# RMSNorm and matmul on one core: weight chunks on the queue of the token loads, first pair of tiles multiplied chunk by chunk

## The chip, the cores and the metric

The kernel runs on one core of one Trainium2 chip. The metric is device time in microseconds (us), the median of several executions. The engines that matter are TensorE (PE in the profile, with its weight loads as PEld), VectorE (DVE), ScalarE (ACT), GpSimd (POOL) and SyncE (SP), which here only issues transfers. "ACTq" and "SPq" are the queues on which ACT and SP issue theirs.

## The reference

```
batch, seq, dim, out_dim = 16, 1024, 512, 768
rms = np.sqrt(np.mean(x ** 2, axis=-1, keepdims=True) + eps)
x_norm = x / rms * gamma
return np.matmul(x_norm, weight).astype(np.float32)
```

`x` holds 16,384 tokens of 512 numbers, `weight` is 512 x 768, all in float32.

## The kernel before, in words

**Tiles.** 128 tokens make a tile, two tiles a pair (64 pairs, numbered j), two pairs a group (32 groups, numbered g). One load brings a group (`xt`, 1 MB), one store takes a group's results away (`ot`, 1.5 MB). The 512 of `dim` is K = 4 chunks of 128; the weight comes in four chunks of 128 rows (`w_f`, 384 KB each). The 768 output columns are two matmuls, of 512 and of 256.

**A pair.** `cast(j)` on POOL turns the pair into bf16 (`xb`). `squares(j)` on ACT sums the squares of both tiles and takes the root (`rms`); DVE then takes the reciprocal (`rstd`). `transposes(j)` is eight transposes on PE into PSUM (`tp`) and one copy by DVE to SBUF (`xT`). `matmuls(j)` multiplies: for each of the two tiles t, for each chunk k, two matmuls with `xT` held and the scaled weight `w_bf` streamed, added up in a PSUM tile `ops`. When a tile is finished, its PSUM is multiplied by `rstd` into `ot`: by ACT for t = 0 (L110), by DVE for t = 1 (L112). This multiplication is called the eviction here.

**The weight.** gamma is loaded as a row (`g_row`), transposed on PE and copied (`g_sb`); four DVE instructions (L148) then scale each weight chunk by gamma into `w_bf` in bf16. Each waits for its chunk to land.

**What sets the order.** Every engine runs its instructions in the order in which the program is written; nothing reorders them. All loads of `x` and all stores are issued by SP; the gamma row and the four weight chunks are issued by ACT (L123, L126). The main loop (L151) issues, for pair j: the load of the group six ahead (j even), `cast(j+2)`, `squares(j+1)`, `transposes(j+1)`, `matmuls(j)`, and after an odd j the store of the group. So pair 1 is squared and transposed ahead of `matmuls(0)`. There are eight `xt` buffers, three of `xb`, three of `xT`, two of `tp`, three of `ops` and four of `ot`; a group's first eviction therefore needs the store of the group four before to have landed. Transfers take eight completion semaphores (DMAHW0 to DMAHW7) in turn, so each transfer from the ninth on also waits until the one eight issues before it has landed.

Of the kernel before, what the change touches and what calls it, by code (L numbers as in the profile page):

```python
# [12 lines left out]
F32 = mybir.dt.float32  # L13
# [4 lines left out]
@with_exitstack  # L18
def kernel(
    ctx: ExitStack,  # L20
    tc: tile.TileContext,
    x: bass.AP,
    gamma: bass.AP,
    weight: bass.AP,
    eps: float,
    out: bass.AP,
):
    nc = tc.nc
    P = 128

    x = x.flatten_outer_dims()
    out = out.flatten_outer_dims()
    N, D = x.shape
    _, O = out.shape
    K = D // P
    G = 4
    NG = N // (P * G)
    NP = 2 * NG
    PF = 6
    SPLITS = [(0, 512), (512, O)]  # L40


    xg = x.rearrange("(g p t) d -> g p t d", p=P, t=G)
    og = out.rearrange("(g p t) o -> g p t o", p=P, t=G)

    singles = ctx.enter_context(tc.tile_pool(name="singles", bufs=1))
    xin = ctx.enter_context(tc.tile_pool(name="xin", bufs=PF + 2))
    xbp = ctx.enter_context(tc.tile_pool(name="xb", bufs=3))
    junk = ctx.enter_context(tc.tile_pool(name="junk", bufs=2))
    stats = ctx.enter_context(tc.tile_pool(name="stats", bufs=4))  # L50
    xt_pool = ctx.enter_context(tc.tile_pool(name="xt", bufs=3))
    tpsum = ctx.enter_context(tc.tile_pool(name="tpsum", bufs=2, space=bass.MemoryType.PSUM))
    opsum = ctx.enter_context(tc.tile_pool(name="opsum", bufs=3, space=bass.MemoryType.PSUM))
    outp = ctx.enter_context(tc.tile_pool(name="out", bufs=4))

    x_tiles, xb_tiles, rstd_tiles, xT_tiles, o_tiles = {}, {}, {}, {}, {}

    def load(g, parts=1):
        xt = xin.tile([P, G, D], F32, name="xt")
        x_tiles[g] = xt  # L60
        n = G // parts
        for i in range(parts):
            nc.sync.dma_start(out=xt[:, i * n:(i + 1) * n, :], in_=xg[g, :, i * n:(i + 1) * n, :])

    def xpair(j):
        return x_tiles[j // 2][:, 2 * (j % 2):2 * (j % 2) + 2, :]

    def cast(j):
        xb = xbp.tile([P, 2, D], BF16, name="xb")
        xb_tiles[j] = xb  # L70
        nc.gpsimd.tensor_copy(out=xb, in_=xpair(j))  # L71

    def squares(j):
        ssq = stats.tile([P, 2], F32, name="ssq")
        for t in range(2):
            jk = junk.tile([P, D], BF16, name="jk")
            nc.scalar.activation(out=jk, in_=xpair(j)[:, t, :], func=AF.Square,  # L77
                                 accum_out=ssq[:, t:t + 1])
        rms = stats.tile([P, 2], F32, name="rms")
        nc.scalar.activation(out=rms, in_=ssq, func=AF.Sqrt, scale=1.0 / D, bias=eps_sb)  # L80
        rstd = stats.tile([P, 2], F32, name="rstd")
        nc.vector.reciprocal(out=rstd, in_=rms)  # L82
        rstd_tiles[j] = rstd

    def transposes(j):
        xb = xb_tiles.pop(j)
        tp = tpsum.tile([P, 2, K, P], BF16, name="tp")
        for t in range(2):
            for k in range(K):
                nc.tensor.transpose(out=tp[:, t, k, :], in_=xb[:, t, k * P:(k + 1) * P], identity=ident)  # L90
        xT = xt_pool.tile([P, 2, K, P], BF16, name="xT")
        nc.vector.tensor_copy(out=xT, in_=tp)  # L92
        xT_tiles[j] = xT

    def matmuls(j):
        g, h = j // 2, j % 2
        if h == 0:
            o_tiles[g] = outp.tile([P, G, O], F32, name="ot")
        ot = o_tiles[g]
        xT = xT_tiles.pop(j)  # L100
        rstd = rstd_tiles.pop(j)
        for t in range(2):
            ops = opsum.tile([P, 2, 512], F32, name="ops").rearrange("p a b -> p (a b)")
            for k in range(K):
                for lo, hi in SPLITS:
                    nc.tensor.matmul(out=ops[:, lo:hi], lhsT=xT[:, t, k, :], rhs=w_bf[:, k, lo:hi],  # L106
                                     start=(k == 0), stop=(k == K - 1))
            dst = ot[:, 2 * h + t, :]
            if t == 0:
                nc.scalar.mul(out=dst, in_=ops[:, :O], mul=rstd[:, t:t + 1])  # L110
            else:
                nc.vector.tensor_single_scalar(out=dst, in_=ops[:, :O], scalar=rstd[:, t:t + 1],  # L112
                                               op=mybir.AluOpType.mult)

    def store(g, lo=0, hi=G):
        nc.sync.dma_start(out=og[g, :, lo:hi, :], in_=o_tiles[g][:, lo:hi, :])

    with tc.manual_schedule():
        nc.scalar.preload_act_table(AF.Sqrt)  # L119
        load(0, parts=2)  # L120

        g_row = singles.tile([K, P], F32)
        nc.scalar.dma_start(out=g_row, in_=gamma.rearrange("(ko ki) -> ko ki", ki=P))  # L123
        w_f32 = singles.tile([P, K, O], F32)
        for k in range(K):
            nc.scalar.dma_start(out=w_f32[:, k, :], in_=weight[k * P:(k + 1) * P, :])  # L126
        for g in range(1, PF):
            load(g)

        ident_f = singles.tile([P, P], F32)  # L130
        make_identity(nc, ident_f)
        ident = singles.tile([P, P], BF16)
        nc.vector.tensor_copy(out=ident, in_=ident_f)  # L133
        eps_sb = singles.tile([P, 1], F32)
        nc.vector.memset(eps_sb, float(eps))

        cast(0)
        cast(1)
        squares(0)
        transposes(0)  # L140

        gp = tpsum.tile([P, K], F32, name="tp")
        nc.tensor.transpose(out=gp, in_=g_row, identity=ident_f[:K, :K])  # L143
        g_sb = singles.tile([P, K], F32)
        nc.vector.tensor_copy(out=g_sb, in_=gp)  # L145
        w_bf = singles.tile([P, K, O], BF16)
        for k in range(K):
            nc.vector.tensor_single_scalar(out=w_bf[:, k, :], in_=w_f32[:, k, :], scalar=g_sb[:, k:k + 1],  # L148
                                           op=mybir.AluOpType.mult)

        for j in range(NP):  # L151
            if j % 2 == 0 and j // 2 + PF < NG:
                load(j // 2 + PF)
            if j + 2 < NP:
                cast(j + 2)
            if j + 1 < NP:
                squares(j + 1)
                transposes(j + 1)
            matmuls(j)
            g = j // 2  # L160
            if g == NG - 1:
                store(g, 2 * (j % 2), 2 * (j % 2) + 2)
            elif j % 2:
                store(g)
# [35 lines left out]
```

## Time and profile before

| what | value |
|---|---|
| median of 3 runs | 222.38 us (222.13 to 222.49) |
| the profiled execution | 222.73 us |
| its span, first to last instruction | 221.0 us |
| outside the span | 1.73 us |
| PE busy | 198.6 us (90%) |
| ACT busy | 156.1 us (71%) |
| DVE busy | 116.1 us (53%) |
| POOL busy | 67.3 us (30%) |
| moved by DMA | 85.73 MB, mean 388 GB/s |
| granted TensorE clock, mean | 0.996 |

Times inside the span count from its start. A row of the timeline has the start, the duration, the engine, the line, the operation, the tiles written and read, the shapes, and how many instructions were merged; in brackets stands how long the engine had been idle, and what ended that. Durations of merged rows run from the first start to the last end. A row of the windows view has the busy time and the instruction count of each engine in one stretch of time, then the granted TensorE clock, the busy share of the DMA engines, and the GB/s moved.

### The profile page before, as it was taken

The page shows a single profiled execution, that of the slowest core. Times are in us where ns is not written, and L with a number is a line of the kernel's source. Part 1 is how long each engine was busy: PE and PEld are TensorE (multiplying, and loading weights), DVE is VectorE, ACT ScalarE, POOL GpSimd, SP SyncE. Part 2 cuts the span into 40 slices and gives each one's busy share as a digit, 9 for nine tenths or more (in the row PEclk, how much of TensorE's full clock was granted, in tenths as well). Part 3 has the DMA queues.
Part 4 walks back from the last instruction along what each step waited for, and adds up shares of the span by engine and source line. Part 5 has one row for each costly group of instructions (what it writes and reads, how often), then busy time and mean ns, then how long its engine had stood idle before and what let it go on. Part 6 is the DMA issues. An engine that isn't in the chain of part 4 may idle for free.

```text
span 221.0 us, 4062 instructions
## 1 busy us (share of the span) xinstructions
PE 198.6 (90%) x1508; PEld 130.8 (59%) x1537; DVE 116.1 (53%) x199; ACT 156.1 (71%) x385; POOL 67.3 (30%) x70
## 2 busy tenths in 40 slices
PE   0514999999999999999999999999999999999990
PEld 0302666666666666666666666666666666666660
DVE  0222356655566555665555665556655566555551
ACT  3501577787777887778877778777788777887750
POOL 2440133322333323333233333233332333322000
PEclk9999999999999999999999999999999999999998
DMA  6999379999999999999999999999999999776767
GB/s 199 420 420 425 151 279 395 417 424 423 422 412 428 427 416 429 421 416 420 426 430 426 423 427 429 428 421 426 429 421 425 426 428 415 336 307 291 291 288 285
DMA packets 10108, 85.73 MB, mean 388 GB/s; under 512 B 1124, under 2 KB 1128, under 8 KB 2152
## 3 DMA queue, kind: packets, MB, share of 16 engines
q1 hardware_dynamic: 9504, 83.89, 91.1%
q10 hardware_dynamic: 584, 1.58, 1.8%
q8 instruction: 12, 0.20, 0.3%
q14 instruction: 8, 0.07, 0.1%
HBM read 35.13 MB, written 50.33 MB: 387 GB/s over the span
## 4 chain that ended last, share of the span: by engine, by line
PE 88%; DMA 7%; issue 1%; DVE 1%; ACTq 1%; ACT 0%
PE ops L106 75%; PE tp L90 13%; DMA w_f<-in_weight_dram 7%; ACTq L126 1%; DVE ot L112 0%; DVE w_bf L148 0%; ACT L119 0%
## 5 line engine op out<-in xcount | busy, mean ns | idle before, releaser
L106 PE MATMUL ops<-w_bf,xT 128*128 128x256 bf16 (+1 forms) x995 | 178.4, 328 | 10.3 <-DVE w_bf L148 8.8
L106 PEld LDWEIGHTS <-xT 128*128 128x128 bf16 x1024 | 98.3, 99 | 69.3 <-issue 12.0
L71 POOL CAST xb<-xt 128x1024 bf16<-128x1024 f32 x64 | 66.6, 1042 | 134.6 <-PE tp L90 125.9
L112 DVE TENSOR_SCALAR ot<-ops,rstd 128x768 f32<-128x768 f32 x64 | 65.1, 1018 | 74.3 <-PE ops L106 74.3
L110 ACT ACTIVATE ot<-ops,rstd 128x768 f32<-128x768 f32 x64 | 57.7, 901 | 53.3 <-PE ops L106 53.3
L77 ACT ACTIVATE jk<-xt 128x512 bf16<-128x512 f32 x128 | 78.7, 619 | 3.1 <-DMA xt<-in_x_dram 3.1
L90 PE MATMUL tp<-ident,xb 128*128 128x128 bf16 x512 | 40.3, 223 | 6.8 <-POOL xb L71 6.2
L90 PEld LDWEIGHTS <-xb 128*128 128x128 bf16 x512 | 34.9, 100 | 15.0 <-POOL xb L71 6.7
L92 DVE COPY xT<-tp 128x1024 bf16<-128x1024 bf16 x64 | 43.0, 671 | 0.3 <-PE tp L90 0.3
L77 ACT ACTIVATION_READ_ACCUMULATOR jk<-xt 128x1 f32 x128 | 24.4, 190 | 0.0
L80 ACT ACTIVATE rms<-ssq,eps_sb 128x2 f32<-128x2 f32 x64 | 18.9, 295 | 2.1
L82 DVE RECIPROCAL rstd<-rms 128x2 f32<-128x2 f32 x64 | 10.6, 166 | 15.1 <-ACT rms L80 15.1
L148 DVE TENSOR_SCALAR w_bf<-w_f,g_sb 128x768 bf16<-128x768 f32 x4 | 2.5, 620 | 9.6 <-DMA w_f<-in_weight_dram 9.6
L119 ACT ACT_TABLE_LOAD x1 | 1.3, 1283 | 0.7 <-PEq L181 0.7
L133 DVE CAST ident<-ident_f 128x128 bf16<-128x128 f32 x1 | 0.2, 228 | 1.3 <-POOL ident_f masks.py:199 1.3
masks.py:199 POOL TENSOR_SCALAR_AFFINE_SELECT ident_f<-ident_f 128x128 f32<-128x128 f32 x1 | 0.3, 294 | 0.1
L143 PEld LDWEIGHTS tp<-ident_f,g_row 4*128 4x128 f32 x1 | 0.2, 178 | 0.2 <-issue 0.2
masks.py:197 POOL MEMSET ident_f<- 128x128 f32 x1 | 0.2, 205 | 0.3 <-POOLq L181 0.3
L143 PE MATMUL tp<-ident_f,g_row 4*128 4x4 f32 x1 | 0.3, 264 | 0.0
L181 POOL MEMSET const-float32-0.0<- 128x1 f32 x1 | 0.1, 99 | 0.2 <-issue 0.2
L145 DVE COPY g_sb<-tp 128x4 f32<-128x4 f32 x1 | 0.2, 152 | 0.0
L181 POOL MEMSET const-bfloat16-1.0<- 128x1 bf16 x1 | 0.1, 102 | 0.0
(3 smaller groups left out, 0.3 us busy)
## 6 DMA issues: line engine op xcount, KB each, us to landing
out_dram<-ot SPq DMA_DIRECT2D x31, 1536.0 KB, 9.7
xt<-in_x_dram SPq DMA_DIRECT2D x31, 1024.0 KB, 12.0
w_f<-in_weight_dram ACTq DMA_DIRECT2D x4, 384.0 KB, 12.3
out_dram<-ot SPq DMA_DIRECT2D x2, 768.0 KB, 3.6
xt<-in_x_dram SPq DMA_DIRECT2D x2, 512.0 KB, 4.9
g_row<-in_gamma_dram ACTq DMA_DIRECT2D x1, 2.0 KB
```

What stands on the lines that cost most here:

```text
L71: nc.gpsimd.tensor_copy(out=xb, in_=xpair(j))
L77: nc.scalar.activation(out=jk, in_=xpair(j)[:, t, :], func=AF.Square, accum_out=ssq[:, t:t + 1])
L80: nc.scalar.activation(out=rms, in_=ssq, func=AF.Sqrt, scale=1.0 / D, bias=eps_sb)
L82: nc.vector.reciprocal(out=rstd, in_=rms)
L90: nc.tensor.transpose(out=tp[:, t, k, :], in_=xb[:, t, k * P:(k + 1) * P], identity=ident)
L92: nc.vector.tensor_copy(out=xT, in_=tp)
L106: nc.tensor.matmul(out=ops[:, lo:hi], lhsT=xT[:, t, k, :], rhs=w_bf[:, k, lo:hi], start=(k == 0), stop=(k == K - 1))
L110: nc.scalar.mul(out=dst, in_=ops[:, :O], mul=rstd[:, t:t + 1])
L112: nc.vector.tensor_single_scalar(out=dst, in_=ops[:, :O], scalar=rstd[:, t:t + 1], op=mybir.AluOpType.mult)
L119: nc.scalar.preload_act_table(AF.Sqrt)
L126: nc.scalar.dma_start(out=w_f32[:, k, :], in_=weight[k * P:(k + 1) * P, :])
L148: nc.vector.tensor_single_scalar(out=w_bf[:, k, :], in_=w_f32[:, k, :], scalar=g_sb[:, k:k + 1], op=mybir.AluOpType.mult)
```

## The change

The four weight chunks are no longer issued by ACT but by SP, between the two halves of the first group: SP issues pair 0's tokens, the four chunks, pair 1's tokens, and then the other groups. The gamma row stays on ACT's queue; its transpose and copy now stand ahead of pair 0's. `matmuls(0)` now comes ahead of `squares(1)` and `transposes(1)`, and its loop runs over chunks outside and over the two tiles inside, with both `ops` tiles open at once. For all other pairs the loop runs as before, except that both `ops` tiles are named ahead of the loop.

```
-        for t in range(2):
-            ops = opsum.tile([P, 2, 512], F32, name="ops").rearrange("p a b -> p (a b)")
-            for k in range(K):
-                for lo, hi in SPLITS:
-                    nc.tensor.matmul(out=ops[:, lo:hi], lhsT=xT[:, t, k, :], rhs=w_bf[:, k, lo:hi],
-                                     start=(k == 0), stop=(k == K - 1))
+        acc = [opsum.tile([P, 2, 512], F32, name="ops").rearrange("p a b -> p (a b)") for _ in range(2)]
+
+        order = [(t, k) for k in range(K) for t in range(2)] if j == 0 else \
+                [(t, k) for t in range(2) for k in range(K)]
+        for t, k in order:
+            for lo, hi in SPLITS:
+                nc.tensor.matmul(out=acc[t][:, lo:hi], lhsT=xT[:, t, k, :], rhs=w_bf[:, k, lo:hi],
+                                 start=(k == 0), stop=(k == K - 1))
+            if k < K - 1:
+                continue
...
-        load(0, parts=2)
...
+        x0 = xin.tile([P, G, D], F32, name="xt")
+        x_tiles[0] = x0
+        nc.sync.dma_start(out=x0[:, 0:2, :], in_=xg[0, :, 0:2, :])
         for k in range(K):
-            nc.scalar.dma_start(out=w_f32[:, k, :], in_=weight[k * P:(k + 1) * P, :])
+            nc.sync.dma_start(out=w_f32[:, k, :], in_=weight[k * P:(k + 1) * P, :])
+        nc.sync.dma_start(out=x0[:, 2:4, :], in_=xg[0, :, 2:4, :])
         for g in range(1, PF):
             load(g)
...
+        gp = tpsum.tile([P, K], F32, name="tp")
+        nc.tensor.transpose(out=gp, in_=g_row, identity=ident_f[:K, :K])
+        g_sb = singles.tile([P, K], F32)
+        nc.vector.tensor_copy(out=g_sb, in_=gp)
+
         cast(0)
         cast(1)
         squares(0)
         transposes(0)
 
-        gp = tpsum.tile([P, K], F32, name="tp")
-        nc.tensor.transpose(out=gp, in_=g_row, identity=ident_f[:K, :K])
-        g_sb = singles.tile([P, K], F32)
-        nc.vector.tensor_copy(out=g_sb, in_=gp)
...
             if j + 2 < NP:
                 cast(j + 2)
+            if j == 0:
+                matmuls(0)
             if j + 1 < NP:
                 squares(j + 1)
                 transposes(j + 1)
-            matmuls(j)
+            if j > 0:
+                matmuls(j)
```

On SP, at the head of the program, the transfers stood in this order before (`xt` are token tiles; 128x1024 is a pair, 128x2048 a group; DMAHW names the completion that is waited for):

```order
L63 DMA xt<-in_x_dram 128x1024 x2
L63 DMA xt<-in_x_dram 128x2048
L63 DMA xt<-in_x_dram 128x2048 [waits DMAHW0_49]
L63 DMA xt<-in_x_dram 128x2048 [waits DMAHW1_49]
L63 DMA xt<-in_x_dram 128x2048 [waits DMAHW2_49]
```

At the same place, with the change:

```order
L130 DMA xt<-in_x_dram 128x1024
L132 DMA w_f_87<-in_weight_dram 128x768 x4
L133 DMA xt<-in_x_dram 128x1024
L63 DMA xt<-in_x_dram 128x2048
L63 DMA xt<-in_x_dram 128x2048 [waits DMAHW0_49]
```

The four weight chunks now lie between the two halves of group 0 on this one queue, and pair 1's half and all later groups lie behind them.

On ACT, up to the eviction of pair 1 (`jk,ssq<-xt` are the squares, two to a pair; `rms` is the root; `ot<-ops,rstd` is the eviction of a pair's first tile), the order before:

```order
L123 DMA g_row<-in_gamma_dram 4x128
L126 DMA w_f_90<-in_weight_dram 128x768 x4
L77 ACTIVATE jk,ssq<-xt 128x512 [waits DMAHW0_49]
L77 ACTIVATE jk,ssq<-xt 128x512
L80 ACTIVATE rms<-ssq,eps_sb 128x2 [waits DVE_49,Activation_49]
L77 ACTIVATE jk,ssq<-xt 128x512 [waits DMAHW2_49]
L77 ACTIVATE jk,ssq<-xt 128x512
L80 ACTIVATE rms<-ssq,eps_sb 128x2 [waits Activation_49]
L110 ACTIVATE ot<-ops,rstd 128x768 [waits DVE_49,PE_49]
```

And with the change:

```order
L125 DMA g_row<-in_gamma_dram 4x128
L77 ACTIVATE jk,ssq<-xt 128x512 [waits DMAHW0_49]
L77 ACTIVATE jk,ssq<-xt 128x512
L80 ACTIVATE rms<-ssq,eps_sb 128x2 [waits DVE_49,Activation_49]
L114 ACTIVATE ot<-ops,rstd 128x768 [waits DVE_49,PE_49]
L77 ACTIVATE jk,ssq<-xt 128x512 [waits DMAHW6_49]
L77 ACTIVATE jk,ssq<-xt 128x512
L80 ACTIVATE rms<-ssq,eps_sb 128x2 [waits Activation_49]
```

The eviction of pair 0, which waits for PE, now stands ahead of pair 1's squares and root. On DVE the same happens: the eviction of pair 0 (L116 in the changed file) stands ahead of pair 1's reciprocal and of its copy to `xT`, where it stood behind them.

More of the change, by code (lines that the diff above doesn't have):

```diff
@@ L101, in matmuls @@
         rstd = rstd_tiles.pop(j)
-        for t in range(2):
-            ops = opsum.tile([P, 2, 512], F32, name="ops").rearrange("p a b -> p (a b)")
-            for k in range(K):
-                for lo, hi in SPLITS:
-                    nc.tensor.matmul(out=ops[:, lo:hi], lhsT=xT[:, t, k, :], rhs=w_bf[:, k, lo:hi],
-                                     start=(k == 0), stop=(k == K - 1))
+        acc = [opsum.tile([P, 2, 512], F32, name="ops").rearrange("p a b -> p (a b)") for _ in range(2)]
[7 more added lines that the diff above has]
+                continue
             dst = ot[:, 2 * h + t, :]
             if t == 0:
-                nc.scalar.mul(out=dst, in_=ops[:, :O], mul=rstd[:, t:t + 1])
+                nc.scalar.mul(out=dst, in_=acc[t][:, :O], mul=rstd[:, t:t + 1])
             else:
-                nc.vector.tensor_single_scalar(out=dst, in_=ops[:, :O], scalar=rstd[:, t:t + 1],
+                nc.vector.tensor_single_scalar(out=dst, in_=acc[t][:, :O], scalar=rstd[:, t:t + 1],
                                                op=mybir.AluOpType.mult)
```

## The prediction

> **What bounds the kernel now.** I read the page's chain of waits first: by engine, and then two pieces of the same chain in order of time (start, duration).
>
> ```profile
> span 221.0 us, 4062 instructions
> PE 88%; DMA 7%; issue 1%; DVE 1%; ACTq 1%; ACT 0%
> ```
>
> ```profile
> 2.98 16.52 DMA w_f<-in_weight_dram
> 20.20 3.35 PE ops L106 x10
> ```
>
> The chain has two parts: until 19.50 us the kernel waits for the weight's transfers, and from 20.20 us to near the end it is PE. Next the windows (busy time and count of each engine, granted clock, DMA share, GB/s):
>
> ```profile
> 5.00:24.00 19.00, 8.43 (x40) 4.73 (x41) 4.47 (x10) 5.65 (x16) 5.15 (x5) 1.00 1.01 418
> 24.50:28.50 4.00, 3.95 (x30) 2.56 (x30) 1.86 (x5) 2.42 (x6) 1.76 (x2) 1.00 0.01 2
> 28.50:29.00 0.50, 0.50 (x5) 0.26 (x3) 0.50 (x2) 0.01 (x1) 0.32 (x1) 1.00 0.00 0
> 34.00:100.00 66.00, 65.47 (x508) 43.45 (x517) 38.31 (x66) 52.12 (x131) 22.80 (x22) 1.00 1.01 421
> 100.00:180.00 80.00, 79.37 (x624) 52.96 (x634) 46.48 (x79) 63.59 (x159) 27.09 (x26) 1.00 1.01 426
> ```
>
> From 34 us PE has no gaps to speak of (65.47 of 66.00), but the DMA engines are full as well; between 24.5 and 29 us they stood still. So there is a second bound close behind PE, to which I come back. Now the timeline of the start:
>
> ```profile
> 5.09 0.63 ACT L77 ACTIVATE jk<-xt 128x512 bf16<-128x512 f32 x1 [3.08 <-DMA xt<-in_x_dram]
> 5.12 1.04 POOL L71 CAST xb<-xt 128x1024 bf16<-128x1024 f32 x1 [3.82 <-DMA xt<-in_x_dram]
> 6.22 1.03 PE L90 MATMUL tp<-ident,xb 128*128 128x128 bf16 x8 [6.22 <-POOL xb L71]
> 6.76 1.04 POOL L71 CAST xb<-xt 128x1024 bf16<-128x1024 f32 x1 [0.60 <-DMA xt<-in_x_dram]
> 7.18 0.26 PE L143 MATMUL tp<-ident_f,g_row 4*128 4x4 f32 x1
> 7.29 0.69 DVE L92 COPY xT<-tp 128x1024 bf16<-128x1024 bf16 x1 [0.34 <-PE tp L90]
> 9.22 0.62 DVE L148 TENSOR_SCALAR w_bf<-w_f,g_sb 128x768 bf16<-128x768 f32 x1 [1.17 <-DMA w_f<-in_weight_dram]
> 10.47 2.03 POOL L71 CAST xb<-xt 128x1024 bf16<-128x1024 f32 x2 [2.67 <-DMA xt<-in_x_dram]
> 12.60 0.62 DVE L148 TENSOR_SCALAR w_bf<-w_f,g_sb 128x768 bf16<-128x768 f32 x1 [2.76 <-DMA w_f<-in_weight_dram]
> 14.03 1.04 POOL L71 CAST xb<-xt 128x1024 bf16<-128x1024 f32 x1 [1.52 <-DMA xt<-in_x_dram]
> 16.07 0.62 DVE L148 TENSOR_SCALAR w_bf<-w_f,g_sb 128x768 bf16<-128x768 f32 x1 [2.85 <-DMA w_f<-in_weight_dram]
> 19.53 0.62 DVE L148 TENSOR_SCALAR w_bf<-w_f,g_sb 128x768 bf16<-128x768 f32 x1 [2.83 <-DMA w_f<-in_weight_dram]
> 20.20 3.35 PE L106 MATMUL ops<-w_bf,xT 128*128 128x512 bf16 x10 [2.66 <-DVE w_bf L148]
> 21.03 0.90 ACT L110 ACTIVATE ot<-ops,rstd 128x768 f32<-128x768 f32 x1 [12.64 <-PE ops L106]
> 23.19 0.29 ACT L80 ACTIVATE rms<-ssq,eps_sb 128x2 f32<-128x2 f32 x1
> 23.35 1.06 PE L90 MATMUL tp<-ident,xb 128*128 128x128 bf16 x8
> 24.21 3.00 PE L106 MATMUL ops<-w_bf,xT 128*128 128x512 bf16 x15
> 27.05 0.61 PE L90 MATMUL tp<-ident,xb 128*128 128x128 bf16 x8
> 27.49 2.76 PE L106 MATMUL ops<-w_bf,xT 128*128 128x512 bf16 x16
> 28.10 0.29 ACT L80 ACTIVATE rms<-ssq,eps_sb 128x2 f32<-128x2 f32 x1
> 28.43 0.17 DVE L82 RECIPROCAL rstd<-rms 128x2 f32<-128x2 f32 x1 [0.16 <-ACT rms L80]
> 28.51 0.67 DVE L92 COPY xT<-tp 128x1024 bf16<-128x1024 bf16 x1
> ```
>
> A weight chunk lands every 3.4 us (9.2, 12.6, 16.1, 19.5), while the token loads on the other queue land between them in their own order (5.1, 6.8, 10.5, 14.0). In 3.45 us at 418 GB/s 1.44 MB pass, and a chunk is 0.39 MB: the weight queue gets little more than a quarter of the flow. Two paces of PE show too: from 20.20 to 23.35 us ten matmuls, five pairs of 512 and 256 columns, take 0.63 us a pair; from 27.49 us sixteen take 2.6. The granted clock reads 1.00 in both.
>
> **The change part by part.** I work out when pair 2's matmuls start, since from there on every pair follows at PE's pace:
>
> ```profile
> 30.54 0.38 PE L106 MATMUL ops<-w_bf,xT 128*128 128x512 bf16 x1
> 210.29 5.36 PE L106 MATMUL ops<-w_bf,xT 128*128 128x512 bf16 x31
> ```
>
> The steps 27.49 to 30.54 (pair 3) and 27.49 to 210.29 (pair 62, sixty pairs) both give 3.05 us a pair. Before, pair 2 starts at 27.49.
>
> *Tokens of pair 0.* Nothing ahead of them moves: they are the first transfer on SP before and after. I keep 5.1 us, and cast, transposes and copy end at 7.29 + 0.69 = 7.98. The gamma transpose, put ahead of them on PE and DVE, lies in their idle time; it waits for a 2 KB row that is still the first transfer on ACT's queue. Cover gone, it would cost what its row at 7.18 took, 0.26 us.
>
> *Weights.* On one queue transfers land in the order of issue, as the token loads do. The four chunks, 1.57 MB at 418 GB/s, take 3.76 us: they land at about 6.0, 7.0, 7.9 and 8.9 us. DVE scales them back to back from 7.98 in 0.62 us each; the last is needed at 9.84. So the weight has left the path, and what is late next is the chain of pair 0 itself. Pair 1's tokens land at 10.1 (0.52 MB later) in place of 6.8, group 1 at 12.6 in place of 10.5; both are needed later than that, below. The four issues leave ACT, which idled then, for SP, where later issues shift by about 1.4 us (a store's issue, quoted below, takes 0.35) under transfers that are queued for microseconds: nothing.
>
> *First pair.* PE's first matmul: 7.98 + 0.62 + 0.05 (the DVE end at 20.15 to PE at 20.20) = 8.65. DVE delivers a chunk each 0.62, PE needs 2 x 0.63 for one: PE is the limit, at the slow pace. Tile 0's last pair of matmuls is the seventh; ACT starts its eviction 0.83 after that pair starts (20.20 to 21.03): 8.65 + 6 x 0.63 + 0.83 = 13.26.
>
> *The new wait.* Behind that eviction on ACT now stand pair 1's squares and root, which were done early before, and behind the root stand DVE's reciprocal and `xT` copy, for which PE waits. From eviction to the end of a root is 23.48 - 21.03 = 2.45; from the end of a root at 28.39 to the end of the copy at 29.18 is 0.79, and 0.05 more to PE. So pair 1's matmuls start at 13.26 + 2.45 + 0.79 + 0.05 = 16.55. PE meanwhile ends pair 0 (13.69) and does the transposes of pairs 1 and 2 at the slow 0.86 (23.35 to 24.21): 15.41, and idles 1.1 us. Pair 1's cast is done by 11.2, pair 2's by 13.7: in time. Pair 2's `xT` follows 1.6 us behind pair 1's, well ahead of its use. Pair 2's matmuls start at 16.55 + 3.05 = 19.60.
>
> *Sum.* 27.49 - 19.60 = 7.89 us earlier. The profiled execution took 222.73, of which 1.73 lie outside the span: 214.84. It lay 0.35 above the median, so the median becomes 222.38 - 7.89 = **214.5**. Unknown ends: if PE speeds up soonest, say 3.4 us after 8.65, 1.67 pairs of the seven save 0.3 each, 0.5 in all; if pair 0's tokens land up to 1.0 us sooner, without a second queue's issues beside them, that comes on top: 213.0.
>
> *The second bound.* Stores:
>
> ```profile
> 28.35 0.35 SPq L116 DMA_DIRECT2D out_dram<-ot  x1
> DMA to landing us min/median/max: 6.9/8.6/9.0
> DMA to landing us min/median/max: 13.5/13.6/13.7
> 47.27 0.90 ACT L110 ACTIVATE ot<-ops,rstd 128x768 f32<-128x768 f32 x1 [0.60 <-PE ops L106]
> ```
>
> Store 0 is issued at 28.35, and group 4's first eviction, which needs its buffer, comes at 47.27: a store has 18.9 us to land. It takes 6.9 us at first and 13.7 at most (issues from 28 to 60 us, and from 174 to 182). Before, store 0 met DMA engines that had nothing to do. After, it is issued 7.9 us sooner, at about 20.5, while the loads ahead of it, the same bytes as before, still end at about 24.5. So the stream of stores starts some 4.5 us sooner than the 29 us of before, and everything is asked for 7.9 sooner: landings grow by about 3.5 us, to 17.2 at the worst. That is 1.7 us inside the limit, and at the end the stores drain, so I add nothing.
>
> **The rivals.**
>
> *The stores take over.* Past 18.9 us ACT's eviction waits, then PE, and the pace is DMA's: 2.62 MB a group (1 MB in, 1.5 MB out) at 421 to 426 GB/s is 6.22 to 6.15 us, where PE needs 2 x 3.05 = 6.09. Over the 24 groups with loads that is 1.4 to 3.1 us at worst: 215.9 to 217.6. For it speaks the thin margin, against it that my estimate stays inside.
>
> *PE stays slow.* Before, the fast pace came only after 24.21, with PE busy without a break from 20.20. If the 1.1 us gap ahead of pair 1 puts that off, pair 1 runs at 8 x 0.63 = 5.0 in place of 2.6, and one set of transposes at 0.86 in place of 0.45: 2.9 us, 217.4. Against it: 16.55 lies 7.9 us after 8.65, and PE will have been idle for 1.1 of them. [...]
>
> *The weights land no sooner.* If sharing between transfers does not depend on the queue, the last chunk still lands at 19.5. Its pair of tile 0 starts at 20.20, pair 1's matmuls at 21.03 + 3.29 = 24.32, against 24.21: the gain is gone, and with PE idle again ahead of it, pair 1 runs slow: 5.0 against the 2.84 of before (24.21 to 27.05, where the next transposes began), plus 0.4 for transposes: about 2.6 slower, **225.0**; with the fast pace in time, 222.5, no change. The change loses from the point at which the last chunk lands after 19.4. [...] Against it stand the landing times above, where each queue lands in its own order and two queues share by turns.
>
> **How the numbers follow.** Forecast, 213.0 to 215.5: 0.70. Stores: 0.11. Slow PE: 0.13. Weights no sooner: 0.05, of which 0.03 slower. The rest is unforeseen. The range goes from 213.2, most of the way to the early ends, to 217.4, the slow pair. A difference under 0.2%, 0.44 us, is about what a measurement of this kernel can't tell from no change: faster 0.95, same 0.02, slower 0.03.
>
> **What would show it.** Right: `w_f` landings below 1 us apart and all before 10 us; the first L108 matmul near 8.7; ACT idle until about 13.3, then its first eviction; a PE gap of about 1 us before pair 1 near 16.5, ended by DVE's `xT`; 3.05 us a pair from 19.6 on; no DMA pause near 25 us; store landings up to 17. Wrong: weight waits on DVE past 10 us; L108 matmuls over 0.6 us after 17; evictions that wait for `out_dram`.

## The result, and the profile after

The change makes the kernel faster: 215.03 us against 222.44, a ratio of 0.9686 with an interval of 0.9635 to 0.9736. One of the four executions took 216.75 us and the other three 214.83 to 215.10, and among the experiments below one execution of "PE kept busy" took 216.80 and one of "earlier still" 360.39 us, both left out of their ratios; why these took longer stays open. The profiled execution took 215.10 us, 7.63 less than the one before.

The page after the change, span and chain by engine:

```profile
span 213.2 us, 4093 instructions
PE 92%; DMA 2%; DVE 1%; ACT 1%; POOL 0%; issue 0%
```

The transfers' share of the chain went from 7% to 2%, and PE's from 88% to 92%. The longest early pieces of the chain in order of time:

```profile
0.74 4.84 DMA xt<-in_x_dram
9.06 4.33 PE ops L108 x14
16.71 2.77 PE ops L108 x16
```

What is left of the transfers is the first token load; the weight's transfers are gone from the chain. The same windows as before the change:

```profile
5.00:24.00 19.00, 14.03 (x95) 8.62 (x96) 8.54 (x17) 10.39 (x28) 8.05 (x8) 1.00 1.01 416
24.50:28.50 4.00, 4.00 (x32) 2.58 (x31) 1.77 (x3) 3.37 (x8) 1.04 (x1) 1.00 1.00 421
34.00:100.00 66.00, 66.00 (x524) 43.63 (x523) 38.31 (x66) 52.60 (x132) 22.58 (x22) 1.00 1.01 426
```

PE is busy for 14.03 us of the first window in place of 8.43, and the DMA engines no longer stop between 24.5 and 28.5 us (421 GB/s in place of 2). Now the timeline of the start:

```profile
5.60 0.63 ACT L77 ACTIVATE jk<-xt 128x512 bf16<-128x512 f32 x1 [3.58 <-DMA xt<-in_x_dram]
7.79 0.69 DVE L92 COPY xT<-tp 128x1024 bf16<-128x1024 bf16 x1 [0.34 <-PE tp L90]
8.40 2.20 DVE L156 TENSOR_SCALAR w_bf<-w_f,g_sb 128x768 bf16<-128x768 f32 x4
9.06 4.64 PE L108 MATMUL ops<-w_bf,xT 128*128 128x512 bf16 x16 [1.31 <-DVE w_bf L156]
13.42 0.90 ACT L114 ACTIVATE ot<-ops,rstd 128x768 f32<-128x768 f32 x1 [6.16 <-PE ops L108]
13.54 0.61 PE L90 MATMUL tp<-ident,xb 128*128 128x128 bf16 x8
13.74 1.02 DVE L116 TENSOR_SCALAR ot<-ops,rstd 128x768 f32<-128x768 f32 x1 [3.14 <-PE ops L108]
14.36 0.62 PE L90 MATMUL tp<-ident,xb 128*128 128x128 bf16 x8 [0.21 <-POOL xb L71]
15.57 0.29 ACT L80 ACTIVATE rms<-ssq,eps_sb 128x2 f32<-128x2 f32 x1
15.90 0.17 DVE L82 RECIPROCAL rstd<-rms 128x2 f32<-128x2 f32 x1 [1.14 <-ACT rms L80]
15.98 0.67 DVE L92 COPY xT<-tp 128x1024 bf16<-128x1024 bf16 x1
16.71 2.77 PE L108 MATMUL ops<-w_bf,xT 128*128 128x512 bf16 x16 [1.73 <-DVE xT L92]
19.77 2.76 PE L108 MATMUL ops<-w_bf,xT 128*128 128x512 bf16 x16
202.56 2.65 PE L108 MATMUL ops<-w_bf,xT 128*128 128x512 bf16 x15
```

The four scalings of the weight are one merged row, back to back from 8.40: none waits for a chunk. Pair 0's matmuls run from 9.06, pair 1's start at 16.71 after PE waited 1.73 us for DVE's `xT`, and behind that wait one reads its chain upwards: copy at 15.98, reciprocal at 15.90, root at 15.57, and the eviction at 13.42 ahead of it on ACT. Pair 2 starts at 19.77, pair 62 at 202.56: 3.05 us a pair, as before. Last, landings of the four weight chunks, and of the stores issued from 20 to 52 us and from 165 to 175:

```profile
DMA to landing us min/median/max: 5.3/6.1/6.9
```

```profile
DMA to landing us min/median/max: 9.4/10.2/10.2
```

```profile
DMA to landing us min/median/max: 14.6/14.7/14.9
```

The chunks, issued from 1.2 to 2.6 us, land from 6.5 to 9.5, in the order of issue; the last landed at 19.5 before.

### The profile page after: what moved, and what is told of

The parts are those of the page before. It is cut to its first block, busy times and chain, and to the rows that moved or that the text cites. A ratio compares the mean times of both kernels' runs of the same rounds, so it can differ in the third digit from the quotient of the medians.

```text
span 213.2 us, 4093 instructions
## 1 busy us (share of the span) xinstructions
PE 198.2 (93%) x1537; PEld 129.9 (61%) x1537; DVE 116.0 (54%) x199; ACT 156.0 (73%) x385; POOL 67.2 (32%) x70
## 4 chain that ended last, share of the span: by engine, by line
PE 92%; DMA 2%; DVE 1%; ACT 1%; POOL 0%; issue 0%
PE ops L108 79%; PE tp L90 13%; DMA xt<-in_x_dram 2%; ACT jk L77 1%; POOL xb L71 0%; DVE ot L116 0%; ACT ot L114 0%; DVE xT L92 0%; DVE w_bf L156 0%; ACT rms L80 0%; DVE rstd L82 0%
## 5 line engine op out<-in xcount | busy, mean ns | idle before, releaser
L108 PE MATMUL ops<-w_bf,xT 128*128 128x512 bf16 (+1 forms) x1024 | 178.6, 328 | 3.0 <-DVE xT L92 1.7
L116 DVE TENSOR_SCALAR ot<-ops,rstd 128x768 f32<-128x768 f32 x64 | 65.1, 1018 | 73.9 <-PE ops L108 73.9
L90 PE MATMUL tp<-ident,xb 128*128 128x128 bf16 x512 | 39.5, 220 | 4.4 <-POOL xb L71 4.4
L90 PEld LDWEIGHTS <-xb 128*128 128x128 bf16 x512 | 34.1, 99 | 12.7 <-POOL xb L71 4.7
## 6 DMA issues: line engine op xcount, KB each, us to landing
out_dram<-ot SPq DMA_DIRECT2D x31, 1536.0 KB, 11.1
```

What stands on the lines that cost most here:

```text
L108: nc.tensor.matmul(out=acc[t][:, lo:hi], lhsT=xT[:, t, k, :], rhs=w_bf[:, k, lo:hi], start=(k == 0), stop=(k == K - 1))
L116: nc.vector.tensor_single_scalar(out=dst, in_=acc[t][:, :O], scalar=rstd[:, t:t + 1], op=mybir.AluOpType.mult)
```

## The experiments

All times are medians; the ratio is to the kernel before the change, run beside on the same chip.

**Only the queue.** The kernel before, with the weight chunks on SP's queue.

```
-        load(0, parts=2)
+        nc.sync.dma_start(out=x0[:, 0:2, :], in_=xg[0, :, 0:2, :])
-            nc.scalar.dma_start(out=w_f32[:, k, :], in_=weight[k * P:(k + 1) * P, :])
+            nc.sync.dma_start(out=w_f32[:, k, :], in_=weight[k * P:(k + 1) * P, :])
+        nc.sync.dma_start(out=x0[:, 2:4, :], in_=xg[0, :, 2:4, :])
```

> Only the weight chunks are moved to SP's queue, between the two halves of group 0; the order of the program and the loops stay as before the change. My theory: the gain is the earlier landing of the weights, and the new order of pair 0 adds little. Pair 1's tokens land at about 10.7, its transposes end at 12.7 on PE ahead of pair 0's matmuls, these run from 12.7 to about 17, pair 2's matmuls start at about 20.3 (19.8 to 21.2) against 19.77 with the whole change: 215.5 us (215.0 to 216.5). Rival: the early weights are of use only with pair 0's matmuls ahead of pair 1's tokens, so that most of the gain is missing: 218 or more.

Measured: 215.75 us, 0.9701 (0.967 to 0.9732). Its PE rows at the start:

```profile
12.19 1.03 PE L90 MATMUL tp<-ident,xb 128*128 128x128 bf16 x8 [4.32 <-POOL xb L71]
13.02 4.21 PE L106 MATMUL ops<-w_bf,xT 128*128 128x512 bf16 x16
17.52 2.76 PE L106 MATMUL ops<-w_bf,xT 128*128 128x512 bf16 x16
```

PE idles 4.3 us for pair 1's tokens, which now lie behind the weight, and then runs through pair 0 and pair 1 (17.52) without another wait. The queue alone brings 6.7 of the 7.4 us; the rest of the change adds 0.7 by the medians. The rival falls.

**Only the order.** The changed kernel with the chunks back on ACT's queue.

```
-            nc.sync.dma_start(out=w_f32[:, k, :], in_=weight[k * P:(k + 1) * P, :])
+            nc.scalar.dma_start(out=w_f32[:, k, :], in_=weight[k * P:(k + 1) * P, :])
```

> The new order of the program and the loop over chunks, but the weight chunks stay on ACT's queue. My theory: the chunks land 3.4 us apart up to 19.5 as before, pair 1's matmuls start at about 24.3 against 24.21 before the change, so nothing is gained: 222.5 us, up to 225 if PE runs pair 1 at the slow pace. Rival: the order brings the gain by itself, since PE works on both tiles while it waits: 217 or less.

Measured: 224.42 us, 1.0092 (1.0066 to 1.0118): slower than before the change. Its rows around the last chunk:

```profile
19.44 0.62 DVE L156 TENSOR_SCALAR w_bf<-w_f,g_sb 128x768 bf16<-128x768 f32 x1 [2.83 <-DMA w_f<-in_weight_dram]
21.35 1.91 PE L90 MATMUL tp<-ident,xb 128*128 128x128 bf16 x16
24.24 5.04 PE L108 MATMUL ops<-w_bf,xT 128*128 128x512 bf16 x16 [0.98 <-DVE xT L92]
29.57 2.76 PE L108 MATMUL ops<-w_bf,xT 128*128 128x512 bf16 x16
```

The chunks land as the prediction's third rival has them: the last chunk at 19.4, pair 1 at 24.24 after a PE gap (24.32 worked out there) and at the slow pace, 5.04 us (5.0), so that pair 2 starts at 29.57 against 27.49. It shows both what two queues do to the weight and what the new order costs when the weight is late. What passes on the two queues can be counted in the trace of the kernel before: from 10 to 18 us it has 305 token packets of 8 KB and 282 weight packets of 3 KB, so that the weight gets 0.26 of the bytes.

**Tile by tile.** The whole change, but pair 0 in the usual loop order.

```
-        order = [(t, k) for k in range(K) for t in range(2)] if j == 0 else \
-                [(t, k) for t in range(2) for k in range(K)]
+        order = [(t, k) for t in range(2) for k in range(K)]
```

> The whole change, except that pair 0's matmuls run tile by tile (all chunks of tile 0, then of tile 1) as in all other pairs. My theory: the weights are ready every 0.62 us and PE takes 0.63 us for one chunk of one tile at the slow pace, so PE waits for no chunk in either order; tile by tile, tile 0 is finished 1.65 us sooner (11.8 in place of 13.4), ACT gets to pair 1's squares sooner, and DVE's eviction of tile 1 (13.7 to 14.8) becomes the last ahead of pair 1's reciprocal: pair 1's matmuls at 15.55 in place of 16.71, 1.2 us gained: 213.9 us. Rival: running chunk by chunk is what lets PE start early, and without it PE waits for the weights: slower than the change, 216 or more.

Measured: 213.84 us, 0.9612 (0.9582 to 0.9643), in its profiled execution a span of 211.8 us. Its first eviction and the matmuls of pairs 1 and 2:

```profile
11.77 0.90 ACT L113 ACTIVATE ot<-ops,rstd 128x768 f32<-128x768 f32 x1 [4.57 <-PE ops L107]
15.27 2.77 PE L107 MATMUL ops<-w_bf,xT 128*128 128x512 bf16 x16
18.32 2.44 PE L107 MATMUL ops<-w_bf,xT 128*128 128x512 bf16 x14
```

The eviction comes at 11.77 as worked out, pair 2 at 18.32 in place of 19.77. Running pair 0 chunk by chunk costs 1.45 us at pair 2 and 1.4 of the span; it is not a source of the gain.

**Squares first.** The whole change, with pair 0's evictions (now a function of their own) issued behind pair 1's squares, root and copy.

```
             if j == 0:
-                matmuls(0)
+                acc0 = matmuls(0)
             if j + 1 < NP:
                 squares(j + 1)
                 transposes(j + 1)
+            if j == 0:
+                evict(0, 0, acc0)
+                evict(0, 1, acc0)
```

> The whole change, except that the evictions of pair 0 stand behind pair 1's squares, root, reciprocal and copy on ACT and DVE. My theory: PE's 1.7 us gap ahead of pair 1 is the wait for that root, which stood behind pair 0's eviction; with it gone, pair 1's matmuls start when pair 2's transposes end, 14.85 in place of 16.71: 213.2 us. Rival: the gap has another cause, or the time is lost again at the next pair: 215 us as with the change.

Measured: 213.89 us, 0.961 (0.9579 to 0.9642), span 211.8 us.

```profile
14.49 0.62 PE L90 MATMUL tp<-ident,xb 128*128 128x128 bf16 x8 [0.93 <-POOL xb L71]
14.95 2.76 PE L106 MATMUL ops<-w_bf,xT 128*128 128x512 bf16 x16
18.00 2.76 PE L106 MATMUL ops<-w_bf,xT 128*128 128x512 bf16 x16
```

The gap's cause is settled: pair 1 starts at 14.95 (14.85 expected), right behind pair 2's transposes, and pair 2 at 18.00, 1.77 sooner than with the change. But the span is only 1.4 shorter; 0.7 us less was gained than expected. The end is taken up below.

**Three output buffers.** The whole change, with less room for stores.

```
-    outp = ctx.enter_context(tc.tile_pool(name="out", bufs=4))
+    outp = ctx.enter_context(tc.tile_pool(name="out", bufs=3))
```

> The whole change, with three output buffers in place of four. A group's first eviction then needs the store of the group three before, so a store has 12.8 us to land in place of 18.9. My theory: stores are the second bound, close behind PE; with the change they take 9.4 us to land at first and 14.9 at most, pass 12.8 from about 118 us on, and from there evictions wait and PE with them, by about 14.9 - 12.8 = 2.1 us in all: 217.1 us. Rival: the stores' landing is not on PE's path at all at these sizes: 215.0.

Measured: 215.71 us, 0.9693 (0.967 to 0.9716); span 213.8 against 213.2. PE's pair 0, then ACT's evictions and PE's pairs late in the run:

```profile
8.90 5.28 PE L108 MATMUL ops<-w_bf,xT 128*128 128x512 bf16 x16 [1.31 <-DVE w_bf L156]
```

```profile
168.67 0.90 ACT L114 ACTIVATE ot<-ops,rstd 128x768 f32<-128x768 f32 x1 [1.56 <-DMA out_dram<-ot]
174.99 0.90 ACT L114 ACTIVATE ot<-ops,rstd 128x768 f32<-128x768 f32 x1 [1.53 <-DMA out_dram<-ot]
```

```profile
181.40 2.76 PE L108 MATMUL ops<-w_bf,xT 128*128 128x512 bf16 x15
184.61 2.77 PE L108 MATMUL ops<-w_bf,xT 128*128 128x512 bf16 x16
187.67 2.76 PE L108 MATMUL ops<-w_bf,xT 128*128 128x512 bf16 x15
191.01 2.77 PE L108 MATMUL ops<-w_bf,xT 128*128 128x512 bf16 x16
```

The waits for stores are there, 1.5 us in each group, and put ACT's evictions 6.32 us apart from one group to the next (168.67 to 174.99), against 6.09. But PE hardly follows: its pairs keep their 3.05 us up to 181.40, and it loses 0.16 us ahead of 184.61 and 0.29 ahead of 191.01. Another 0.16 of the 0.6 us comes from the start, where all of pair 0 ran at the slow pace (5.28 us in place of 4.64) and pair 2 began at 19.93 in place of 19.77. So the stores cost about 0.45 us, not 2.1. The second bound is real and much softer than I took it to be; that the third PSUM tile lets PE run on meanwhile is my reading and was not tried.

**PE kept busy.** The whole change, with 58 matmuls of the identity in PE's idle time.

```
+        def keep_busy(n):
+            for _ in range(n):
+                nc.tensor.matmul(out=idle[:, :P], lhsT=ident, rhs=ident, start=True, stop=True)
+        keep_busy(44)
         gp = tpsum.tile([P, K], F32, name="tp")
...
         transposes(0)
+        keep_busy(14)
```

> The whole change, with 58 more matmuls of the identity with itself on PE in its idle time: 44 ahead of the gamma transpose and 14 behind pair 0's transposes; their result is not used. My theory: PE's slow pace at the start comes from PE having idled, so pair 0 now runs at the fast pace: its transposes take 0.45 in place of 0.86, its first eviction comes at about 11.1 in place of 13.4, pair 1's root follows at 13.5, and pair 1's matmuls start when pair 2's transposes end, at about 14.9 in place of 16.7. As with the evictions moved, the stores at the end keep a part of that: 213.6 us. Rival: the slow pace is that of the first microseconds after the start, whatever PE does: 215.0.

Measured: 213.42 us, 0.961 (0.9579 to 0.9642).

```profile
1.61 4.88 PE L148 MATMUL ops<-ident 128*128 128x128 bf16 x44 [1.61 <-DVE eps_sb L142]
6.66 0.62 PE L90 MATMUL tp<-ident,xb 128*128 128x128 bf16 x8
8.59 2.76 PE L108 MATMUL ops<-w_bf,xT 128*128 128x512 bf16 x15 [0.53 <-DVE w_bf L164]
11.07 0.90 ACT L114 ACTIVATE ot<-ops,rstd 128x768 f32<-128x768 f32 x1 [3.86 <-PE ops L108]
14.97 2.76 PE L108 MATMUL ops<-w_bf,xT 128*128 128x512 bf16 x16
```

Pair 0's transposes take 0.62 in place of 1.03 and its matmuls 2.76 in place of 4.64; the first eviction comes at 11.07 (11.1 expected). With PE busy from 1.61 us the fast pace is there at 6.66 us, where with the change the transposes at 6.72 still took 1.03: here the slow pace goes with PE's idle time, not with the first microseconds.

**Tokens first.** The whole change, with both halves of group 0 ahead of the weight.

```
         nc.sync.dma_start(out=x0[:, 0:2, :], in_=xg[0, :, 0:2, :])
+        nc.sync.dma_start(out=x0[:, 2:4, :], in_=xg[0, :, 2:4, :])
         for k in range(K):
             nc.sync.dma_start(out=w_f32[:, k, :], in_=weight[k * P:(k + 1) * P, :])
-        nc.sync.dma_start(out=x0[:, 2:4, :], in_=xg[0, :, 2:4, :])
```

> The whole change, with both halves of group 0 ahead of the weight chunks on SP's queue. In the runs with weight chunks right behind them, pair 0's tokens landed at 5.45 to 5.58 us, in the two with pair 1's tokens behind them at 4.77 and 5.07. My theory: what follows on the queue delays them by about 0.5 us; here they land at about 5.0, the chunks at 7.7 to 10.6, which is still ahead of PE's need, and pair 1's matmuls start some 0.5 us sooner, at 16.2: 214.5 us. Rival: the difference is chance: 5.5 us, 215.0.

Measured: 214.2 us, 0.9641 (0.9607 to 0.9675).

```profile
4.77 0.63 ACT L77 ACTIVATE jk<-xt 128x512 bf16<-128x512 f32 x1 [2.75 <-DMA xt<-in_x_dram]
16.20 2.77 PE L108 MATMUL ops<-w_bf,xT 128*128 128x512 bf16 x15 [1.40 <-DVE xT L92]
```

Pair 0's tokens land at 4.8 us in place of 5.6, although they are the first transfer either way; pair 1 starts at 16.20 in place of 16.71. In all kernels with a token half behind them they landed at 4.7 to 5.1, with a weight chunk behind them at 5.4 to 5.6. That the follower delays them is shown; by what means is open.

**Earlier still, and all of it.** First (e9) the busy PE, the evictions of pairs 0 and 1 behind the next pair's squares, and pair 1's matmuls ahead of pair 2's transposes:

```
-            if j == 0:
-                matmuls(0)
+            if j < 2:
+                acc = matmuls(j)
             if j + 1 < NP:
                 squares(j + 1)
                 transposes(j + 1)
+            if j < 2:
+                evict(j, 0, acc)
+                evict(j, 1, acc)
```

> The whole change, with the extra matmuls that keep PE busy, with the evictions of pairs 0 and 1 behind the squares, roots and copies of the next pair, and with pair 1's matmuls ahead of pair 2's transposes. Pair 2's matmuls should start at about 17.2 us, against 19.8 with the change and 18.0 with pair 0's evictions moved alone. My theory: with these moves the transfers set the end, since all bytes at 426 GB/s from 2.5 us on leave no more to gain; the last store still lands at about 211 us of the span: 213.6 us. Rival: PE still sets the end, and the 0.8 us against the moved evictions comes in full: 213.0 or less.

Then (e10) the same kernel with both token halves ahead of the weight, as above:

> The kernel with the extra matmuls, the evictions of pairs 0 and 1 behind the next pair's squares, roots and copies, and pair 1's matmuls ahead of pair 2's transposes (e9), now with both halves of group 0 ahead of the weight chunks on SP's queue. Pair 0's tokens should land at 4.8, pair 1's matmuls start near 12.9 and pair 2's near 16.7, against 17.8 in e9, so PE should be through about 1.0 us sooner (last eviction on ACT at 203.4 in place of 204.45). My theory: the stores now set the end, since their queue no longer runs empty before PE is through: the last store still lands at about 210.4 of the span, and the time from the last ACT eviction to it grows from 5.93 to nearly 7: 213.1 us. Rival: PE still sets the end: 5.7 us from the last eviction to the last landing, 209.1 of the span, 211.9 us.

Measured: 213.16 us, 0.9581 (0.9559 to 0.9603), and 212.76 us, 0.9562 (0.953 to 0.9593), the fastest of this study. Pair 2 starts later than worked out, at 17.5 and 17.0 in place of 17.2 and 16.7. In e9 pair 1 waits for its `xT` until 13.53, and in e10 the 44 extra matmuls hold up pair 0's transposes; in both pair 2's transposes now stand behind pair 1's matmuls, and PE waits once more for their copy, so that pair 2 starts 4.0 us behind pair 1. The last eviction on ACT, in the order PE kept busy, e9, e10:

```profile
204.92 0.90 ACT L114 ACTIVATE ot<-ops,rstd 128x768 f32<-128x768 f32 x1 [1.70 <-PE ops L108]
```

```profile
204.45 0.90 ACT L118 ACTIVATE ot<-ops,rstd 128x768 f32<-128x768 f32 x1 [1.70 <-PE ops L106]
```

```profile
203.91 0.90 ACT L118 ACTIVATE ot<-ops,rstd 128x768 f32<-128x768 f32 x1 [1.70 <-PE ops L106]
```

And the landing of the last store in these three, issued at 207.30, 206.83 and 206.30:

```profile
DMA to landing us min/median/max: 3.3/3.3/3.3
```

```profile
DMA to landing us min/median/max: 3.6/3.6/3.6
```

```profile
DMA to landing us min/median/max: 3.8/3.8/3.8
```

PE is through 1.0 us sooner in e10 than with PE kept busy alone, the last store only 0.5 (210.1 against 210.6). Neither theory holds as put: the stores don't fix the end, and PE's gain doesn't come in full. With ACT's last eviction in e9 and e10 ahead of 204.5 us, the last store takes longer than the 3.3 us that it takes with the change, which I read as a queue that isn't empty yet. In squares first it took 3.7 us too, and that is 0.4 of what was missing there. But ACT's last eviction (204.90) and the last issue (207.3) stand there as they do with PE kept busy, whose last store took 3.3: the time at which ACT ends does not decide alone, and what else does is open.

## Why the prediction was right

Each step, in us from the start of the span; the last row is the whole time, with what lies outside the span:

| step | worked out | measured |
|---|---|---|
| pair 0's tokens | 5.1 | 5.6 |
| last weight chunk lands | 8.9 | 9.5 |
| first matmul | 8.65 | 9.06 |
| first eviction | 13.26 | 13.42 |
| pair 1's matmuls | 16.55 | 16.71 |
| pair 2's matmuls | 19.60 | 19.77 |
| pace after that, a pair | 3.05 | 3.05 |
| worst landing of a store | 17.2 | 14.9 |
| span | 213.11 | 213.2 |
| profiled execution | 214.84 | 215.10 |

The median came out at 215.03 where 214.5 was forecast. About 0.1 us of that lies in the span and 0.16 outside it (1.89 us in place of 1.73); the rest is that the profiled execution lay 0.35 above its median before and 0.07 now.

The mechanism is the one forecast: on one queue the chunks land in the order of issue, 1.0 us apart, the weight leaves the chain, and the chain of pair 0 and PE's pace set the time. The queue alone shows that it is the landing that pays, and the order alone that the rest doesn't pay without it.

- *Pair 0's tokens* were mis-sized, and my bound pointed the wrong way: I allowed for a landing up to 1.0 sooner, and it came 0.5 later. Tokens first shows why: it is the chunk that follows on the queue, and with tokens there they landed at 4.8 in place of 5.6.
- *The slow pace* ended sooner than it did before. The first eviction at 13.42 is 4.36 us behind the first matmul, where seven slow pairs would have given 4.61: the fast pace began within pair 0, and that gave back 0.25 of the 0.4 by which the first matmul was late (9.06 for 8.65). That it did was luck: with three output buffers, where the first matmul came at 8.90, pair 0 was slow to its end. PE kept busy confirms what the term is made of. I read the granted clock wrongly: in both traces the record of the clock begins only where the fast pace does, at 12.91 us with the change and at 24.69 before, so the 1.00 that the views print for the time ahead of that stands for no record. By these records the fast pace came 3.85 us behind pair 0's first matmul with the change, and before it 4.49 us behind the matmul at 20.20. In the other runs the length of pair 0's sixteen matmuls tells it: 4.64 us with the change, 4.48 tile by tile, 4.21 with only the queue, 4.18 in squares first, and 5.28, slow to the end, with three output buffers and with tokens first. No run shows the 3.4 us behind the first matmul that the early end of the range counts on. What the runs showed in its place is a time that changes from run to run: the 4.18 of squares first is 1.1 us short of the slow 5.28, which at 0.3 us saved a pair puts the start of the fast pace at about 2.8 us, my estimate from these rows, and where it is 5.28 no pair was saved. The later gap of 1.73 us did not bring the slow pace back: pair 1 took 2.77 us behind it.
- *The new wait* was right in place and cause; squares first takes it away. PE's gap was 1.73 rather than 1.1 mainly because the transposes ahead of it ran at the fast pace; its end moved by only 0.16.
- *The stores* were mis-sized. I took the stream of stores to start 4.5 us sooner and landings to grow by 3.5; the first grew by 2.5 (6.9 to 9.4), the worst by 1.2 (13.7 to 14.9). What I left out is that before the change less was moved behind the pause too:

```profile
29.00:34.00 5.00, 4.95 (x42) 3.42 (x42) 2.61 (x5) 4.37 (x11) 1.17 (x2) 1.00 0.99 350
```

The kernel before moved 350 GB/s in these 5 us (393, 381 and 397 in the first three of them, 332 and 246 in the last two, with the DMA engines busy for 0.99 of the time; why is open), and 421 up to 100 us. The changed one moved 433 in the same 5 us, and 426 after. At 426 GB/s what the kernel before fell short by in these two stretches is 0.9 and 0.8 us, most of the 2.3 by which I had the worst landing grow too much. Three output buffers shows besides that ACT's waits for stores reach PE late and in small part, so passing the limit would have cost less than I priced it at.

- *The third rival*, weights that land no sooner, was priced at 225.0; with the chunks left on ACT's queue it took 224.42. With the program the same otherwise, the chunks landed 3.4 us apart on ACT's queue and 1.0 apart on SP's, so the landing does depend on the queue here.

## What to carry to other kernels

When a start-up wait is a small transfer that shares the engines with a large prefetch, look at which queue it is on before the order of the computation: on a queue of its own it got 0.26 of the bytes here, a chunk each 3.4 us, and on the prefetch's queue, ahead of it, a chunk landed each 1.0 us. When work is moved ahead of other work, read what stands behind it on every engine that it uses: here an eviction, put ahead of the next pair's root, held PE up for 1.7 us. And before a loop is turned to follow data as it lands, check that the data is the slower side.

## What the runs showed of the hardware

- PE showed two paces: a matmul of 512 columns and one of 256 took 0.63 us together behind an idle stretch and 0.33 later, and eight transposes 0.86 and 0.45. Matmuls with no use, run through the idle time, brought the fast pace forward (2.76 us for pair 0 in place of 4.64). The views print a granted clock of 1.00 for both; the matmul times tell them apart.
- The fast pace did not come at a fixed time behind the first matmul: by the traces' records of the clock 4.49 us behind the matmul at 20.20 before and 3.85 behind the one at 9.06 with the change, and pair 0's sixteen matmuls took 4.18 to 5.28 us in the six kernels listed above. What sets the time is not shown.
- With transfers waiting on two queues, the kernel before moved 305 packets of 8 KB on one and 282 of 3 KB on the other in 8 us (10 to 18 us).
- The first transfer on SP's queue landed later with weight chunks (packets of 3 KB) behind it, at 5.4 to 5.6 us in seven runs, than with tokens (packets of 4 KB) behind it, at 4.7 to 5.1 in four. Why is open.
- In the 5 us behind its pause the kernel before moved 350 GB/s with the DMA engines busy for 0.99 of them, against 433 in the same 5 us without the pause.
